# Where the operands of a split-float32 matmul lie in SBUF: two neighbouring x tiles in one block, high and low parts in blocks of their own, one distance to the weights modulo 256 bytes

## The chip, the cores and the metric

The kernel runs on one core of one Trainium2 chip. The metric is the device time of one execution in microseconds (us), the median of several runs. Nothing else runs on the chip's other cores.

## The reference

One inference step of a one-layer hybrid decoder trunk, 256 prompt tokens and 32 sample tokens (8 sequences of 4), model width 2048, float32 throughout. Both groups of tokens go through the same weights:

```
def swiglu(x, w_in, w_out):
    gate, up = jnp.split(x @ w_in, 2, axis=-1)
    return (jax.nn.silu(gate) * up) @ w_out
...
x = x + 0.5 * rmsnorm(swiglu(rmsnorm(x, g[0]), ffn1_w_in[l], ffn1_w_out[l]), g[1])
m, sg, sh = hybrid_mixer(rmsnorm(x, g[2]), mix_w_in[l], ..., mix_w_out[l], s_gla[l], s_hgrn[l])
x = x + rmsnorm(m, g[3])
x = x + 0.5 * rmsnorm(swiglu(rmsnorm(x, g[4]), ffn2_w_in[l], ffn2_w_out[l]), g[5])
```

The two feed-forward layers have 2048 x 11264 and 5632 x 2048 weights each. The mixer has an input projection of 7184 columns, two linear recurrences (gated linear attention and HGRN2), and an output projection of 2048 x 2048. The matrix products with these weights are nearly all of the arithmetic.

## The kernel before

**Layout.** Activations lie transposed: a tile `x{k}` holds 128 of the 2048 model features (partitions) by 288 tokens (256 prompt, 32 sample). There are 16 such tiles (KT = 16), and as many products along the contraction.

**Split float32.** TensorE multiplies in a rounded float32 form (`F32R`). To keep float32 accuracy each operand is split into a high part (the value rounded by a copy on ScalarE, ACT) and a low part (the remainder, by VectorE, DVE). A product of weight tile w and activation tile x is then three matmuls that add up in the same PSUM bank, in `mm3` of `block` (lines 617 to 619): w high by x high (L617), w high by x low (L618), w low by x high (L619). I call these three a triple, and one matmul a product. Each product has a weight load of its own (128 columns of 128 weights) and streams 288 columns of x. In all there are 16,152 such products: the groups `gate` and `up` (feed-forward input), `out` (feed-forward output, which streams the hidden parts `hp` instead of `xp`), and in the mixer `qk`, `v`, `hfq`, `hi`, `gate` and `mo`.

**Loops.** `block` runs over units of weights; a unit is 128 x 1024 weights, that is two neighbouring tiles k by 512 output columns. Within a unit it goes over four output groups f of 128 columns, and for each over the two k: so the triples run (k even, f 0), (k odd, f 0), (k even, f 1), (k odd, f 1), and so on: 24 products per unit. In the first blocks of each stage some units run with k outside (`byk`).

**Weights.** `Weights.load` brings a unit by one DMA of the SP queue into one of three raw buffers; `pieces` splits it, ACT writes the high part (L119), DVE the low part (L120), into a buffer `wh` of `[128, 2, 1024]`: for each k 512 high values, then 512 low values. There are four such buffers in the pool `hlp`. Around the borders between stages two more lie in an extra pool (`hx2`, `hx4`) at the right end of SBUF, and `wider` gives them every third pair of units there: 80 of the 1,408 triples of `out` and 144 triples of x tiles take their weights from these, counted in the built program.

**Activations as moving operand.** `pair` makes for each k a tile of `[128, 4, 2, 72]` values: the 288 tokens are cut into four places of 72, and in each place 72 high values are followed by 72 low values. `turns_of` makes the matmul read it in turns: 4 values (16 bytes) of place 0, 4 of place 1, of place 2, of place 3, then the next 4 of place 0. Two places lie 576 bytes apart, so the four reads of a turn lie 64 bytes apart modulo 256. The low part starts 288 bytes behind the high part, which is 32 modulo 256. `do_in` makes the same layout for four tiles of hidden units (`hp`).

**Gaps.** Small unused tiles (`gap_w`, `gap_f`, `{name}gap`, `gap{gnext}`) shift where the pools start. With them the start addresses are, modulo 256, in bytes: x high 64, x low 96; hidden high 192, hidden low 224; weights in `hlp` 96, in the extra pools 224. All x tiles are 2304 = 9 x 256 bytes, all weight offsets are multiples of 512, so these numbers hold for every k, f and buffer.

**Order.** The order of instructions on each engine is laid down by the kernel's code; TensorE goes through the products one after another, and loads the weights of the next product while it streams the present one.

Of the kernel before, what the change touches and what calls it, by code (L numbers as in the profile page):

```python
# [9 lines left out]
F32 = mybir.dt.float32  # L10
F32R = mybir.dt.float32r
# [5 lines left out]
P = 128  # L17
TP = 256
TS = 32
T = TP + TS  # L20
# [3 lines left out]
KT = D // P  # L24
# [6 lines left out]

RAW_BUFS = 3
HL_BUFS = 4
HALF = 1024
LINE = 4
PLACES = 4


def columns(t):

    return t.rearrange("p (g c) -> p g c", g=PLACES)
# [4 lines left out]
    return t.rearrange("p g (i e) -> p i g e", e=LINE)  # L46


def pair(pool, name):

    t = pool.tile([P, PLACES, 2, T // PLACES], F32R, name=name)
    return t[:, :, 0, :], t[:, :, 1, :]

SCAN_LAG = 4
X_EARLY = 12
# [2 lines left out]
class Weights:  # L58
# [46 lines left out]
    def pieces(self, n):  # L105

        i = self.split
        raw = self.raws.pop(i)
        pool = self.extra if i in self.extra_units else self.hlp
        hl = pool.tile([P, 2, HALF], F32R, name=f"wh{i}", tag="wh")  # L110
        h, l = hl[:, :, 0:512], hl[:, :, 512:1024]
        self.parts[i] = (h, l)
        self.split += 1
        raw = raw.rearrange("p (a b) -> p a b", b=512)
        for j in range(n):
            a = slice(0, 2) if n == 1 else slice(2 * j // n, 2 * j // n + 1)
            w = min(512, 1024 // n)
            c = slice(j * w % 512, j * w % 512 + w)
            i1 = self.nc.scalar.activation(h[:, a, c], raw[:, a, c], AF.Copy).ins  # L119
            i2 = self.nc.vector.tensor_tensor(l[:, a, c], raw[:, a, c], h[:, a, c].bitcast(F32), op=ALU.subtract).ins  # L120
            self.recent = i1, i2
            yield i1, i2
# [27 lines left out]
def trunk_kernel(ctx, tc, x_prompt, x_sample, state_gla, state_hgrn, norm_gains, f1_in, f1_out, f2_in, f2_out,  # L150
# [6 lines left out]
    xpool = ctx.enter_context(tc.tile_pool(name="xpool", bufs=1))  # L157
    rawp = ctx.enter_context(tc.tile_pool(name="rawp", bufs=RAW_BUFS))
    hlp = ctx.enter_context(tc.tile_pool(name="hlp", bufs=HL_BUFS))
    hlp.tile([P, 24], F32, name="gap_w", bufs=1)  # L160
    mmp = ctx.enter_context(tc.tile_pool(name="mmp", bufs=5, space=PSUM))
    aux = ctx.enter_context(tc.tile_pool(name="aux", bufs=3, space=PSUM))
    sqp = ctx.enter_context(tc.tile_pool(name="sqp", bufs=2))
# [18 lines left out]
    def act(out, in_, func, **kw):  # L182
        act_set(func)
        ins = S.activation(out, in_, func, **kw).ins
        order(ins, cur["load"])
        cur["users"].append(ins)
        return ins
# [39 lines left out]
    def wider(n):  # L227

        return {i for i in range(n - 44, n + 4) if i // 2 % 3 == (n + 2) // 2 % 3}
# [37 lines left out]
    EARLY = 4  # L267
    x = [xpool.tile([P, T], F32, name=f"x{k}") for k in range(KT)]
    yg = [xpool.tile([P, 4, T], F32, name=f"y{k}") for k in range(4)]
    y = [yg[k // 4][:, k % 4, :] for k in range(KT)]  # L270
    xh, xl = zip(*(pair(xpool, f"xp{k}") for k in range(KT)))
    rt = xpool.tile([P, T], F32, name="rt")
    rp = xpool.tile([P, T], F32, name="rp")
    acc = xpool.tile([P, T], F32, name="acc")
# [223 lines left out]
    class PreNorm:  # L498
# [3 lines left out]
        def __init__(self, name, update, ahead, at):  # L502

            self.name, self.update, self.ahead, self.at, self.late = name, update, ahead, at, []
            self.tmps = None
# [25 lines left out]
    class Fill:  # L531
# [2 lines left out]

        def __init__(self, pool, name, gains, gnext, some, ahead):
            self.gnext, self.name, self.some, self.ahead = gnext, name, some, ahead
            pool.tile([P, 24], F32, name=f"{name}gap")

            self.tiles = [[pair(pool, f"{name}{n}{k}") for k in range(EARLY)] for n in "xy"]
            self.gains = pool.tile([P, 48], F32, name=f"{name}g")[:, 0:EARLY]  # L540
            V.tensor_tensor(self.gains, gains[:, 0:EARLY], prm[:, gnext * KT:gnext * KT + EARLY], op=ALU.mult)

        def old(self):
# [136 lines left out]
    def ffn(tag, gcol, gnext, pn, before, fill=None):  # L680
# [2 lines left out]
        border = []  # L683
        with ExitStack() as pools:
            fp = pools.enter_context(tc.tile_pool(name=f"ffn{tag}", bufs=2))
            fp.tile([P, 8], F32, name=f"gap_f{tag}", bufs=1)
            hid, final_tiles = {}, []

            def do_in(c):
                hp = fp.tile([P, 4, PLACES, 2, T // PLACES], F32R, name=f"hp{tag}_{c}", tag="hp")  # L690
                hh, hl = ([hp[:, f, :, j, :] for f in range(4)] for j in range(2))
                hid[c] = (hh, hl)
                gs = []

                def gate(g):
                    def run():
                        V.tensor_tensor(g, g, rt, op=ALU.mult)
                        act(g, g, AF.Silu)
                    return run

                def ev_gate(f, ps):
                    g = fp.tile([P, T], F32, name="g", tag="g", bufs=6)
                    gs.append(g)
                    if c == 0:
                        W.behind = S.activation(g, ps, AF.Copy).ins
                        pn.late.append(gate(g))
                    else:
                        V.tensor_tensor(g, ps, rt, op=ALU.mult)
                        act(g, g, AF.Silu)

                def ev_up(f, ps):
                    u = fp.tile([P, T], F32, name="u", tag="u", bufs=3)
                    ins = V.tensor_tensor(u, ps, rt, op=ALU.mult).ins  # L713
                    V.tensor_tensor(u, u, gs[f], op=ALU.mult)
                    S.activation(hh[f], columns(u), AF.Copy)
                    V.tensor_tensor(hl[f], columns(u), hh[f].bitcast(F32), op=ALU.subtract)
                    return ins

                if c == 0:
                    block(f"gate{tag}_0", KT, xrhs, ev_gate, tick=pn.tick0, most=1 if final else 0, fill=fill,  # L720
                          late=0 if final else FIRST, byk=range(KT))
                    before.close()
                    if not final:
                        border.append(Border(mixer_start, hg1, gnext, 5, 2))
                else:
                    block(f"gate{tag}_{c}", KT, xrhs, ev_gate, byk=(2,) if c == 1 else ())
                if final and c == 0:
                    last_pool()
                block(f"up{tag}_{c}", KT, xrhs, ev_up, tick=pn.tick1 if c == 0 else None,
                      byk=(0,) if c == 1 or final and c == 0 else (), lag=int(c == 0))  # L730
# [3 lines left out]
            def last_pool():  # L734

                zp = pools.enter_context(tc.tile_pool(name="last", bufs=1, side="right", reuse_waits="tile"))
                for n in ("z", "x"):
                    final_tiles.append((zp.tile([P, KT, 2, P], F32, name=f"{n}T"), zp.tile([P, D // 4], F32, name=f"{n}S")))
                final_tiles.append(zp)
# [92 lines left out]
            for kind, c, n in ffn_ops():  # L832
                do_out(c, n) if kind == "out" else do_in(c)
# [864 lines left out]
    class Border:  # L1698


        def __init__(self, n, gains, gnext, some, ahead=0):
            self.pools = ExitStack()
            top = self.pools.enter_context(tc.tile_pool(name=f"top{gnext}", bufs=1, side="right"))
            top.tile([P, 64], F32, name=f"gap{gnext}")
            W.begin_extra(self.pools.enter_context(tc.tile_pool(name=f"hx{gnext}", bufs=2, side="right")), wider(n))
            self.fill = Fill(self.pools.enter_context(tc.tile_pool(name=f"fl{gnext}", bufs=1, side="right")),
                             f"fill{gnext}", gains, gnext, some, ahead)

    pn = pre1 = PreNorm("pre1", x_first, FIRST, 11)
    pn.late.append(prm2)  # L1710
    u, border = ffn(1, lambda k: hg1[:, k:k + 1], 2, pn, first)
    u, border = mixer(PreNorm("pre2", u, UPDATED, 11), border)
    ffn(2, lambda k: hg1[:, KT + k:KT + k + 1], None, PreNorm("pre3", u, UPDATED, 11), border.pools, border.fill)


# [39 lines left out]
```

## Time and profile before

| | |
|---|---|
| time, median of 3 runs | 2179.05 us (2178.4 to 2179.31) |
| the profiled execution's own time | 2178.23 us |
| its span, first to last instruction | 2176.5 us |
| TensorE matmul (PE) busy | 2166.9 us |
| weight loads on TensorE (PEld) busy | 2148.0 us |
| VectorE (DVE), ScalarE (ACT) busy | 1384.1, 1017.8 us |
| DMA | 384.87 MB, mean 177 GB/s |

PE and PEld are two rows of one engine: loading the next weights overlaps the present product. [...] What a product costs is the spacing from its start to the next one's start; that is read from the times of the timeline, or from the count of matmuls in a stretch. A stretch's count includes those that began before it and had not ended: two, where matmuls of 290 ns follow each other every 127 to 129 ns.

### The profile page before, as it was taken

The page shows a single profiled execution, that of the slowest core. Times are in us where ns is not written, and L with a number is a line of the kernel's source. Part 1 is how long each engine was busy: PE and PEld are TensorE (multiplying, and loading weights), DVE is VectorE, ACT ScalarE, POOL GpSimd, SP SyncE. Part 2 cuts the span into 40 slices and gives each one's busy share as a digit, 9 for nine tenths or more (in the row PEclk, how much of TensorE's full clock was granted, in tenths as well). Part 3 has the DMA queues.
Part 4 walks back from the last instruction along what each step waited for, and adds up shares of the span by engine and source line. Part 5 has one row for each costly group of instructions (what it writes and reads, how often), then busy time and mean ns, then how long its engine had stood idle before and what let it go on. Part 6 is the DMA issues. An engine that isn't in the chain of part 4 may idle for free.

```text
span 2176.5 us, 43224 instructions
## 1 busy us (share of the span) xinstructions
PE 2166.9 (100%) x17828; PEld 2148.0 (99%) x17828; DVE 1384.1 (64%) x2253; ACT 1017.8 (47%) x1537; POOL 180.1 (8%) x327
## 2 busy tenths in 40 slices
PE   9999999999999999999999999999999999999999
PEld 9999999999999999999999999999999999999998
DVE  7645546554565568888888755844555466556656
ACT  6453333343334345655676654544333343333344
POOL 2000000000000001233110000000000020122005
PEclk9999999999999999999999999999999999999999
DMA  7655555555556654678566664555555565666555
GB/s 224 181 169 171 174 172 168 173 173 171 171 174 184 176 174 137 198 208 219 175 192 181 178 189 136 170 171 173 175 168 172 174 181 171 184 185 179 172 170 159
DMA packets 227334, 384.87 MB, mean 177 GB/s; under 512 B 21362, under 2 KB 60864, under 8 KB 227136
## 3 DMA queue, kind: packets, MB, share of 16 engines
q1 hardware_dynamic: 213872, 365.02, 56.6%
q0 software_dynamic: 10992, 16.77, 2.9%
q8 instruction: 140, 2.29, 0.4%
q10 hardware_dynamic: 2272, 0.31, 0.1%
q14 instruction: 58, 0.48, 0.1%
HBM read 363.75 MB, written 11.80 MB: 173 GB/s over the span
## 4 chain that ended last, share of the span: by engine, by line
PE 93%; DVE 3%; DMA 2%; ACT 1%; issue 1%; POOL 0%; ACTq 0%; DVEq 0%; POOLq 0%
PE gate L617 9%; PE gate L618 9%; PE gate L619 9%; PE out L619 8%; PE out L618 8%; PE out L617 8%; PE up L619 8%; PE up L618 8%; PE up L617 8%; PE hfq L617 1%; PE hfq L618 1%; PE hfq L619 1%; PE mo L617 1%; PE mo L619 1%; PE mo L618 1%; DVE wh L120 1%
## 5 line engine op out<-in xcount | busy, mean ns | idle before, releaser
L120 DVE TENSOR_TENSOR wh<-raw,wh 128x1024 fp32r<-128x1024 f32 (+1 forms) x676 | 821.8, 1217 | 591.1 <-ACT wh L119 590.1
L119 ACT ACTIVATE wh<-raw 128x1024 fp32r<-128x1024 f32 (+1 forms) x676 | 710.5, 1052 | 916.3 <-PE gate L619 286.1
L617 PE MATMUL gate<-xp,wh 128*128 128x288 f32 x1660 | 481.2, 291 | 0.5 <-DVE u L713 0.3
L619 PE MATMUL gate<-xp,wh 128*128 128x288 f32 x1660 | 477.5, 289 | 0.0
L618 PE MATMUL gate<-xp,wh 128*128 128x288 f32 x1660 | 476.4, 289 | 0.1
L617 PE MATMUL out<-hp,wh 128*128 128x288 f32 x1408 | 410.9, 292 | 0.0
L618 PE MATMUL out<-hp,wh 128*128 128x288 f32 x1408 | 409.7, 291 | 0.0
L619 PE MATMUL out<-hp,wh 128*128 128x288 f32 x1408 | 409.3, 291 | 0.0
L617 PE MATMUL up<-xp,wh 128*128 128x288 f32 x1408 | 408.1, 290 | 0.0
L619 PE MATMUL up<-xp,wh 128*128 128x288 f32 x1408 | 406.4, 289 | 0.0
L618 PE MATMUL up<-xp,wh 128*128 128x288 f32 x1408 | 406.3, 289 | 0.0
L618 PEld LDWEIGHTS gate<-xp,wh 128*128 128x128 f32 x1660 | 311.1, 188 | 1.0 <-DVE xp L283 0.7
L617 PEld LDWEIGHTS gate<-xp,wh 128*128 128x128 f32 x1660 | 310.6, 187 | 1.4 <-issue 0.5
L619 PEld LDWEIGHTS gate<-xp,wh 128*128 128x128 f32 x1660 | 310.8, 188 | 0.2 <-DVE wh L120 0.2
L619 PEld LDWEIGHTS out<-hp,wh 128*128 128x128 f32 x1408 | 265.5, 189 | 0.0
L618 PEld LDWEIGHTS out<-hp,wh 128*128 128x128 f32 x1408 | 264.9, 188 | 0.0
L618 PEld LDWEIGHTS up<-xp,wh 128*128 128x128 f32 x1408 | 264.7, 188 | 0.0
L617 PEld LDWEIGHTS out<-hp,wh 128*128 128x128 f32 x1408 | 263.9, 187 | 0.3 <-DVE y L804 0.3
L619 PEld LDWEIGHTS up<-xp,wh 128*128 128x128 f32 x1408 | 264.0, 187 | 0.0
L617 PEld LDWEIGHTS up<-xp,wh 128*128 128x128 f32 x1408 | 263.7, 187 | 0.0
L804 DVE TENSOR_TENSOR y<-out,y 128x288 f32<-128x288 f32 x287 | 120.6, 452 | 80.1 <-PE out L619 79.7
L761 POOL DMA_DIRECT2D xT<-b x64 | 37.1, 586 | 746.7 <-PE gate L619 558.9
(417 smaller groups left out, 2549.7 us busy)
## 6 DMA issues: line engine op xcount, KB each, us to landing
raw<-in_ffn_w_in_dram SPq DMA_DIRECT2D x350, 512.0 KB, 3.7
raw<-in_ffn_w_out_dram SPq DMA_DIRECT2D x176, 512.0 KB, 3.7
raw<-in_mix_w_in_dram SPq DMA_DIRECT2D x64, 512.0 KB, 4.3
raw<-in_mix_w_in_dram SPq DMA_DIRECT2D x96, 256.0 KB, 3.3
raw<-in_mix_w_out_dram SPq DMA_DIRECT2D x32, 512.0 KB, 3.6
out_dram<-s POOLq DMA_DIRECT2D x32, 256.0 KB, 3.1
s<-in_state_gla_dram SPq DMA_DIRECT2D x16, 256.0 KB, 5.9
s<-in_state_hgrn_dram SPq DMA_DIRECT2D x16, 256.0 KB, 5.7
```

What stands on the lines that cost most here:

```text
L119: i1 = self.nc.scalar.activation(h[:, a, c], raw[:, a, c], AF.Copy).ins
L120: i2 = self.nc.vector.tensor_tensor(l[:, a, c], raw[:, a, c], h[:, a, c].bitcast(F32), op=ALU.subtract).ins
L617: yield lambda: PE.matmul(dst, w[0][:, a, c], parts[0], start=start, stop=False)
L618: yield lambda: PE.matmul(dst, w[0][:, a, c], parts[1], start=False, stop=False)
L619: yield lambda: PE.matmul(dst, w[1][:, a, c], parts[0], start=False, stop=stop)
L761: queues[n % len(queues)].dma_start(dst[q * TS:(q + 1) * TS, 4 * g:4 * g + 4, :, cols].rearrange("p k t c -> p (k t) c"), b32[rows, q])
L804: V.tensor_tensor(y[k], ps, y[k], op=ALU.add)
```

## The change

The change gives the parts of x, of the hidden units and of the tiles for the stage borders (`Fill`) another layout, and pads the weight buffers.

- `pairs` takes the place of `pair`. All high parts of n tiles lie in one block, all low parts in a second block behind it. Two neighbouring tiles, k even and k odd, share a piece of 2304 bytes: in each of the four places 72 values of the even tile, then 72 values of the odd tile. The low block starts 16 bytes further modulo 256 than the high block.
- The weight buffer's row for one k grows from 1024 to 1032 values (`HALF`), so that the odd k's weights lie 32 bytes further modulo 256, as the odd x tile does.
- The gap tiles get other sizes.

| start modulo 256 bytes | before | after |
|---|---|---|
| low part minus high part, same tile | 32 | 16 |
| weights minus x high, weights in `hlp` / extra | 32 / 160 | 96 / 96 |
| weights minus hidden high, in `hlp` / extra | 160 / 32 | 96 / 96 |
| weights minus the low part, in the same order | 0 / 128, 128 / 0 | 80 / 80, 80 / 80 |
| next triple's weights minus this x high, k even to odd | as above | 128 |
| the same, k odd to even | as above | 64 |

```diff
-HALF = 1024
+HALF = 1024 + 8
...
-def pair(pool, name):
-
-    t = pool.tile([P, PLACES, 2, T // PLACES], F32R, name=name)
-    return t[:, :, 0, :], t[:, :, 1, :]
+def pairs(pool, n, names):
+
+    parts = []
+    for at, name in zip((0, LINE), names):
+        t = pool.tile([P, n * T + 16 * at], F32R, name=name, tag=name.split("_")[0])[:, at:at + n * T]
+        t = t.rearrange("p (k g j c) -> p k g j c", g=PLACES, j=2, c=T // PLACES)
+        parts.append([t[:, k // 2, :, k % 2, :] for k in range(n)])
+    return parts
...
-        hl = pool.tile([P, 2, HALF], F32R, name=f"wh{i}", tag="wh")
+        hl = pool.tile([P, 2112], F32R, name=f"wh{i}", tag="wh")[:, 0:2 * HALF].rearrange("p (a c) -> p a c", a=2)
...
-    hlp.tile([P, 24], F32, name="gap_w", bufs=1)
+    hlp.tile([P, 40], F32, name="gap_w", bufs=1)
...
-    xh, xl = zip(*(pair(xpool, f"xp{k}") for k in range(KT)))
+    xh, xl = pairs(xpool, KT, ("xh", "xl"))
...
-            pool.tile([P, 24], F32, name=f"{name}gap")
-
-            self.tiles = [[pair(pool, f"{name}{n}{k}") for k in range(EARLY)] for n in "xy"]
-            self.gains = pool.tile([P, 48], F32, name=f"{name}g")[:, 0:EARLY]
+            pool.tile([P, 8], F32, name=f"{name}gap")
+
+            self.tiles = [list(zip(*pairs(pool, EARLY, (f"{name}{n}h", f"{name}{n}l")))) for n in "xy"]
+            self.gains = pool.tile([P, 24], F32, name=f"{name}g")[:, 0:EARLY]
...
-            fp.tile([P, 8], F32, name=f"gap_f{tag}", bufs=1)
+            fp.tile([P, 24], F32, name=f"gap_f{tag}", bufs=1)
...
-                hp = fp.tile([P, 4, PLACES, 2, T // PLACES], F32R, name=f"hp{tag}_{c}", tag="hp")
-                hh, hl = ([hp[:, f, :, j, :] for f in range(4)] for j in range(2))
+                hh, hl = pairs(fp, 4, (f"hh{tag}_{c}", f"hl{tag}_{c}"))
...
-            top.tile([P, 64], F32, name=f"gap{gnext}")
+            top.tile([P, 80], F32, name=f"gap{gnext}")
```

The instructions of every engine, their order and their shapes stay the same; addresses differ. One wait is new. On POOL (GpSimd), where the mixer's scratch is set up (`it`, `vs` and `ahl` are scratch tiles, `mi` and `bm` masks), the rows of before are:

```order
L974 DMA mi_9570<-in_masks_dram 128x576 [waits DMASW0_49,PE_49]
L975 DMA bm_9571<-in_masks_dram 96x8 [waits DMASW1_49]
L977 MEMSET it 128x256
L977 MEMSET vs_9300 128x512
L977 MEMSET vs_9298 128x512
```

and in the changed kernel, three lines further down the file:

```order
L977 DMA mi_9563<-in_masks_dram 128x576 [waits DMASW0_49,PE_49]
L978 DMA bm_9564<-in_masks_dram 96x8 [waits DMASW1_49]
L980 MEMSET it 128x256
L980 MEMSET vs_9293 128x512 [waits PE_49]
L980 MEMSET vs_9291 128x512
```

The first `vs` memset now waits for TensorE as the mask DMA three rows ahead of it does, since the scratch tile overlaps another part of the border's tiles.

## The prediction, before the run

> **What bounds the kernel.** I read the page's busy times first, then the chain that ended last, then what TensorE's products are spaced at.
>
> ```profile
> span 2176.5 us, 43224 instructions
> PE 2166.9 (100%) x17828; PEld 2148.0 (99%) x17828; DVE 1384.1 (64%) x2253; ACT 1017.8 (47%) x1537; POOL 180.1 (8%) x327
> PEclk9999999999999999999999999999999999999999
> PE 93%; DVE 3%; DMA 2%; ACT 1%; issue 1%; POOL 0%; ACTq 0%; DVEq 0%; POOLq 0%
> ACT wh L119 <- PE gate L619: 286.1, 147, 2.0
> ```
>
> TensorE is busy all the time, at the full granted clock, and holds 93% of the chain. The last row, from the list of waits, says that the engine that prepares weights waits for products to give buffers back, not the other way round. So the time is the number of products times their spacing, and whatever changes the spacing by one part in a hundred changes the time by nearly as much. The groups of TensorE give the count (here L617, the first of three lines of equal count):
>
> ```profile
> L617 PE MATMUL gate<-xp,wh 128*128 128x288 f32 x1660 | 481.2, 291 | 0.5 <-DVE u L713 0.3
> L617 PE MATMUL out<-hp,wh 128*128 128x288 f32 x1408 | 410.9, 292 | 0.0
> L617 PE MATMUL up<-xp,wh 128*128 128x288 f32 x1408 | 408.1, 290 | 0.0
> L617 PE MATMUL hfq<-xp,wh 128*128 128x288 f32 x256 | 76.0, 297 | 0.0
> L617 PE MATMUL mo<-xp,wh 128*128 128x288 f32 x256 | 74.6, 291 | 0.1
> L617 PE MATMUL hi<-xp,wh 128*128 128x288 f32 x128 | 37.8, 296 | 0.0
> L617 PE MATMUL v<-xp,wh 128*128 128x288 f32 x128 | 37.8, 295 | 0.0
> L617 PE MATMUL qk<-xp,wh 128*128 128x288 f32 x124 | 34.4, 294 | 0.2 <-ACT xp L282 0.2
> ```
>
> With the 16 products of `Fill` these are 5,384 triples, 16,152 products. Now their spacing, from stretches that hold whole blocks (columns: the stretch, its length, PE busy and matmuls, clock, DMA share, GB/s):
>
> ```profile
> 502.75:551.68 48.93, 48.93 (x386) 1.00 0.57 172
> 551.68:576.48 24.80, 24.80 (x194) 1.00 0.57 170
> 576.48:625.45 48.97, 48.97 (x386) 1.00 0.58 172
> 718.03:724.15 6.12, 6.12 (x50) 1.00 0.61 173
> 724.15:773.31 49.16, 49.16 (x387) 1.00 0.58 172
> ```
>
> The first is one `gate` and one `up` block: 386 less the two that began before is 384 products in 48.93 us, 127.4 ns each. The third is the next such pair, 127.5. The second is four `out` blocks, 192 products in 24.80 us: 129.2 ns. Shapes and engines' load differ little; what differs is that x stands 32 bytes below its weights (modulo 256) and the hidden parts 160. The fourth stretch tells these apart: it is an `out` block whose weights lie in the extra pool, distance 32, and 48 products take 6.12 us, 127.5 ns. The fifth is the mirror image: `gate` and `up` with three in eight of their units in the extra pool, distance 160: 384 products in 49.16 us, 128.0, close to 5/8 of 127.5 and 3/8 of 129.2. So **the distance of the weights from the moving operand modulo 256 sets the spacing**, 127.5 ns at 32 and 129.2 at 160, for either operand.
>
> [...]
>
> **Part 1: one distance for all.** Products now at 160 go to the common distance: 1,408 - 80 = 1,328 triples of `out` and 144 of x, 1,472 triples or 4,416 products. If the new distance were as good as 32, each would gain 129.2 - 127.5 = 1.7 ns: 4,416 x 1.7 = 7.5 us. Nothing lies beside it: TensorE is the path.
>
> **Part 2: what the new distance is worth.** The trace has no product at 96 and 80. Its nearest rows are those of `Fill`, whose parts stand 64 below the weights; four triples from the timeline's first to the next block's first product:
>
> ```profile
> 1349.46 0.29 PE L617 MATMUL fill<-fill4y,wh 128*128 128x288 f32 x1
> ...
> 1350.86 0.30 PE L619 MATMUL fill<-fill4y,wh 128*128 128x288 f32 x1
> 1351.00 0.29 PE L617 MATMUL gate<-xp,wh 128*128 128x288 f32 x1
> ```
>
> Eleven steps in 1.40 us are 127.3 ns, twelve in 1.54 are 128.3: 64 is about as good as 32. The layout changes a second thing, which the steps within a stretch bear on:
>
> ```profile
> 510.02 0.29 PE L617 MATMUL gate<-xp,wh 128*128 128x288 f32 x1
> 510.15 0.29 PE L618 MATMUL gate<-xp,wh 128*128 128x288 f32 x1
> 510.27 0.29 PE L619 MATMUL gate<-xp,wh 128*128 128x288 f32 x1
> 510.40 0.29 PE L617 MATMUL gate<-xp,wh 128*128 128x288 f32 x1
> 510.53 0.29 PE L618 MATMUL gate<-xp,wh 128*128 128x288 f32 x1
> 510.66 0.29 PE L619 MATMUL gate<-xp,wh 128*128 128x288 f32 x1
> 510.78 0.29 PE L617 MATMUL gate<-xp,wh 128*128 128x288 f32 x1
> 510.91 0.29 PE L618 MATMUL gate<-xp,wh 128*128 128x288 f32 x1
> 511.04 0.29 PE L619 MATMUL gate<-xp,wh 128*128 128x288 f32 x1
> 511.16 0.29 PE L617 MATMUL gate<-xp,wh 128*128 128x288 f32 x1
> ```
>
> Over three triples the steps from L617 to L618 add to 0.39 us, from L618 to L619 to 0.38, from L619 to the next L617 to 0.37: about 130, 127 and 123 ns, each known to 3 ns by the rounding. The first two stay in one piece of 2304 bytes (a tile's high and low part), the last goes to another tile, and is the shortest. In the changed layout it is the other way round: high and low lie in blocks of their own, so two of three steps leave the piece, while the step from one triple to the next mostly stays in the piece that even and odd tile share. I take 125.5 for a step that leaves (between 123 and 127) and 129.3 for one that stays (between 127 and 130): (2 x 125.5 + 129.3) / 3 = 126.8 ns.
>
> **Bounds:** from 125 ns for all (near the shortest kind of step) to 129.2 (all as at 160). Against 127.5 that is, for 16,152 products, from -40 to +27 us. I take 126.8, -11 us: both nearest rows, 64 and 32, are on the good side, and the share of steps that leave the piece doubles.
>
> **The rest costs nothing.** ACT and DVE write the same elements in rows of another pitch:
>
> ```profile
> L120 DVE TENSOR_TENSOR wh<-raw,wh 128x1024 fp32r<-128x1024 f32 (+1 forms) x676 | 821.8, 1217 | 591.1 <-ACT wh L119 590.1
> L119 ACT ACTIVATE wh<-raw 128x1024 fp32r<-128x1024 f32 (+1 forms) x676 | 710.5, 1052 | 916.3 <-PE gate L619 286.1
> ```
>
> A unit's 24 products take 24 x 127.5 ns = 3.06 us; its split takes 1.05 us on ACT and 1.22 on DVE. If the new addresses made these even a fifth slower, some 0.2 us per unit, the products would still cover it; without that cover 0.2 us on each of 676 pieces would be 135 us. The new wait of POOL's memset is for products that the mask DMA three rows ahead waits for too, at the mixer's border; behind it stand one memset and the loads of the gate weights, and POOL is busy 8% of the span. SP's queue gets nothing new, and at 57% share the DMAs have room for products that come 1% sooner.
>
> **Sum.** The profiled execution took 2178.2 us (span 2176.5 and 1.7 around it). 2178.2 - 7.5 - 11.3 = 2159.4. The median of before is 0.8 us above that execution, so I say **2160 us**, 0.9% faster.
>
> **Rivals.**
> - *The distance 128 decides (slower).* From an even tile to the odd one, the next weights now lie 128 beyond the x that is being streamed. That is the distance of the low parts in `out`, in the stretch at 129.2 ns; and none of the new ones (96, 80, 64) is 32 or 0. If this and the unknown pair cost all products what 160 and 128 cost, the time is 2178.2 + 16,152 x 1.7 ns - 4,416 x 1.7 ns = 2198. It turns to a loss when the mean spacing passes 127.5 + 7.5 us / 16,152 = 128.0 ns. Against it: `Fill` at 64. Chance 0.22.
> - *Nothing happens.* [...] By chance the new spacing may also be 127.7 to 128.2. Together 0.13.
> - *Only part 1.* The new distance is as good as 32 and no better: 2178.2 - 7.5 = 2170.7. Chance 0.2.
> - *All steps become short.* 125 to 126 ns everywhere: 2130 to 2147. Chance 0.1.
> - *The change doesn't do what it says.* 16 tiles of 1152 bytes are 18432 = 72 x 256, so the low block does start 16 bytes off, and 1032 values are 4128 = 16 x 256 + 32. I give this nothing of its own.
>
> My forecast, 126.2 to 127.3 ns or 2150 to 2168, has 0.35.
>
> **How the numbers follow.** Faster by over 0.2% (about what a measurement of this kernel can tell from no change; below 2174.7): the forecast, only part 1, and all short, 0.35 + 0.2 + 0.1 = 0.65. Same: 0.13. Slower: 0.22. The range leaves out the far half of the short case and the far end of the slow one: 2138 to 2197.
>
> **What would show it.** The stretches that hold whole blocks: `gate`, `up` and `out` must stand at one spacing, whatever pool the weights come from (part 1), and at about 126.8 ns (part 2); L617 to L618 must have become shorter, L619 to L617 longer. If the `out` stretch has gained and `gate` lost, the distance to the next weights decides, not the piece. If `gate` and `out` still differ, part 1 is wrong. An idle PE ahead of L617 with DVE or ACT as releaser would mean that the writes have become slower.

## The result, and the profile after

| | before | after |
|---|---|---|
| time, median | 2179.14 us (2178.4 to 2179.31, 4 runs) | 2159.28 us (2157.96 to 2159.76, 4 runs) |
| ratio, 95% interval | | 0.9909 [0.9891, 0.9926] |
| the profiled execution's own time | 2178.23 us | 2157.96 us |

The changed kernel is 0.9% faster: 19.9 us by the medians, 20.3 us between the two profiled executions. These are the rows of its page that answer to those of before: span and busy times, the granted clock in tenths, the chain that ended last, and the two groups that write the split weights (busy us, mean ns of one, idle time ahead).

```profile
span 2156.2 us, 43224 instructions
PE 2144.9 (99%) x17828; PEld 2126.5 (99%) x17828; DVE 1382.0 (64%) x2253; ACT 1017.1 (47%) x1537; POOL 180.6 (8%) x327
PEclk9999999999999999999999999999999999999999
PE 94%; DVE 3%; ACT 2%; DMA 1%; issue 1%; DVEq 0%; ACTq 0%; SPq 0%
L124 DVE TENSOR_TENSOR wh<-raw,wh 128x1024 fp32r<-128x1024 f32 (+1 forms) x676 | 822.1, 1217 | 579.9 <-ACT wh L123 577.7
L123 ACT ACTIVATE wh<-raw 128x1024 fp32r<-128x1024 f32 (+1 forms) x676 | 710.1, 1052 | 899.0 <-PE gate L623 282.5
```

TensorE is still the bound, at the same clock, and the writers take the same 1,217 and 1,052 ns as before. PE's busy time fell by 22.0 us and the span by 20.3: the gain is TensorE's alone. The stretches of whole blocks in the changed kernel (stretch, its length, PE busy and matmuls, clock, DMA share, GB/s), TensorE's rows only:

```profile
498.18:546.82 48.64, 48.64 (x386) 1.00 0.58 173
546.82:571.14 24.32, 24.32 (x194) 1.00 0.59 174
711.07:717.16 6.09, 6.09 (x51) 1.00 0.63 180
717.16:765.80 48.64, 48.64 (x387) 1.00 0.57 173
```

The first is a `gate` and an `up` block, 384 products in 48.64 us; the second four `out` blocks, 192 in 24.32; the third an `out` block from the extra pool, 48 in 6.09 (the ends are rounded to 0.01 us); the fourth `gate` and `up` with three in eight of their units in the extra pool. All stand at 126.7 ns (by its rounded row the third would have 126.9, by its start times it has 126.67), where before had 127.4, 129.2, 127.5 and 128.0. By the start times in the trace it is 126.66 to 126.68 ns in nearly every whole block of the feed-forward layers. Over all steps under 150 ns from one product to the next, the mixer's with them, the mean went from 128.08 to 126.81 ns, and the longer steps add up to 24 us in both kernels. 16,152 x 1.27 ns = 20.5 us is the whole gain.

The steps within the first stretch, from the timeline (L621, L622, L623 are the former L617, L618, L619):

```profile
498.18 0.29 PE L621 MATMUL gate<-xh,wh 128*128 128x288 f32 x1
498.31 0.29 PE L622 MATMUL gate<-xl,wh 128*128 128x288 f32 x1
498.44 0.29 PE L623 MATMUL gate<-xh,wh 128*128 128x288 f32 x1
498.56 0.29 PE L621 MATMUL gate<-xh,wh 128*128 128x288 f32 x1
498.69 0.29 PE L622 MATMUL gate<-xl,wh 128*128 128x288 f32 x1
498.82 0.29 PE L623 MATMUL gate<-xh,wh 128*128 128x288 f32 x1
498.94 0.29 PE L621 MATMUL gate<-xh,wh 128*128 128x288 f32 x1
```

Every triple takes 0.38 us here. The rows seem to say 130, 130 and 120 ns for the three kinds of step, but a triple of 380 ns is a whole number of 10 ns, so the same rounding error comes back in every triple. The trace's own start times give, over the 64 triples of this `gate` block, 127.3, 126.3 and 126.5 ns; for the block shown of before 128.6, 127.5 and 126.1.

### The profile page after: what moved, and what is told of

Its sections match the earlier page's. It is cut to its first block, busy times and chain, and to the rows that moved or that the text cites. A ratio compares the mean times of both kernels' runs of the same rounds, so it can differ in the third digit from the quotient of the medians.

```text
span 2156.2 us, 43224 instructions
## 1 busy us (share of the span) xinstructions
PE 2144.9 (99%) x17828; PEld 2126.5 (99%) x17828; DVE 1382.0 (64%) x2253; ACT 1017.1 (47%) x1537; POOL 180.6 (8%) x327
## 4 chain that ended last, share of the span: by engine, by line
PE 94%; DVE 3%; ACT 2%; DMA 1%; issue 1%; DVEq 0%; ACTq 0%; SPq 0%
PE gate L621 10%; PE gate L622 9%; PE gate L623 9%; PE out L621 8%; PE out L622 8%; PE out L623 8%; PE up L621 8%; PE up L622 8%; PE up L623 8%; PE hfq L621 2%; PE mo L621 1%; PE hfq L622 1%; PE hfq L623 1%; PE mo L623 1%; PE mo L622 1%; ACT wh L123 1%
## 5 line engine op out<-in xcount | busy, mean ns | idle before, releaser
L124 DVE TENSOR_TENSOR wh<-raw,wh 128x1024 fp32r<-128x1024 f32 (+1 forms) x676 | 822.1, 1217 | 579.9 <-ACT wh L123 577.7
L123 ACT ACTIVATE wh<-raw 128x1024 fp32r<-128x1024 f32 (+1 forms) x676 | 710.1, 1052 | 899.0 <-PE gate L623 282.5
L621 PE MATMUL gate<-xh,wh 128*128 128x288 f32 x1660 | 479.8, 290 | 0.6 <-ACT wh L123 0.4
L623 PE MATMUL gate<-xh,wh 128*128 128x288 f32 x1660 | 476.4, 288 | 0.0
L622 PE MATMUL gate<-xl,wh 128*128 128x288 f32 x1660 | 475.6, 289 | 0.1
L621 PE MATMUL up<-xh,wh 128*128 128x288 f32 x1408 | 406.8, 289 | 0.0
L621 PE MATMUL out<-hh,wh 128*128 128x288 f32 x1408 | 406.7, 289 | 0.0
L622 PE MATMUL up<-xl,wh 128*128 128x288 f32 x1408 | 405.9, 288 | 0.0
L622 PE MATMUL out<-hl,wh 128*128 128x288 f32 x1408 | 405.9, 288 | 0.0
L623 PE MATMUL up<-xh,wh 128*128 128x288 f32 x1408 | 405.8, 288 | 0.0
L623 PE MATMUL out<-hh,wh 128*128 128x288 f32 x1408 | 405.7, 288 | 0.0
L621 PEld LDWEIGHTS gate<-xh,wh 128*128 128x128 f32 x1660 | 311.0, 188 | 1.7 <-ACT wh L123 0.6
L622 PEld LDWEIGHTS gate<-xl,wh 128*128 128x128 f32 x1660 | 310.2, 188 | 1.1 <-DVE xl L287 0.8
L623 PEld LDWEIGHTS gate<-xh,wh 128*128 128x128 f32 x1660 | 311.0, 188 | 0.2 <-DVE wh L124 0.2
L623 PEld LDWEIGHTS up<-xh,wh 128*128 128x128 f32 x1408 | 264.3, 188 | 0.0
L623 PEld LDWEIGHTS out<-hh,wh 128*128 128x128 f32 x1408 | 264.3, 188 | 0.0
L621 PEld LDWEIGHTS out<-hh,wh 128*128 128x128 f32 x1408 | 264.2, 188 | 0.0
L621 PEld LDWEIGHTS up<-xh,wh 128*128 128x128 f32 x1408 | 264.2, 188 | 0.0
L622 PEld LDWEIGHTS up<-xl,wh 128*128 128x128 f32 x1408 | 264.1, 188 | 0.0
L622 PEld LDWEIGHTS out<-hl,wh 128*128 128x128 f32 x1408 | 264.0, 188 | 0.0
```

The costliest lines, as they stand in the source:

```text
L621: yield lambda: PE.matmul(dst, w[0][:, a, c], parts[0], start=start, stop=False)
L622: yield lambda: PE.matmul(dst, w[0][:, a, c], parts[1], start=False, stop=False)
L623: yield lambda: PE.matmul(dst, w[1][:, a, c], parts[0], start=False, stop=stop)
```

## The experiments

Two questions stood after the result. Is it the distance to the weights or the layout that pays? And why 126.67 ns? Where a spacing is given to a hundredth of a ns, it is worked out from the start times in the trace of that run. In the kernel's own variants nothing of the computation is left out; the five benchmarks compute nothing of the reference, and each ran once.

### One distance, old layout

Before, with the gaps alone changed, so that all weights lie 32 bytes above the high part and none at 160: part 1 without part 2.

```diff
-            fp.tile([P, 8], F32, name=f"gap_f{tag}", bufs=1)
+            fp.tile([P, 40], F32, name=f"gap_f{tag}", bufs=1)
...
-            top.tile([P, 64], F32, name=f"gap{gnext}")
+            top.tile([P, 32], F32, name=f"gap{gnext}")
```

> The kernel before with its old layout, but the gaps set so that all weights, in both pools, stand 32 bytes above x high and hidden high modulo 256 (part 1 alone; only the 48 products of Fill stand elsewhere). Distance theory (the distance of the next weights from the streamed operand sets the spacing): out falls from 129.2 to 127.5 ns, gate and up stay at 127.5, the time falls by 7.5 us to 2171. Piece theory (a step that stays in a piece of 2304 bytes is long, one that leaves it short): the layout is the old one, so by it alone nothing moves, 2178 to 2179.

Measured: 2169.97 us, ratio 0.9965 [0.9952, 0.9978]. The stretches (`gate` and `up`, then four `out` blocks):

```profile
501.18:550.10 48.92, 48.92 (x386) 1.00 0.58 173
550.10:574.57 24.47, 24.47 (x195) 1.00 0.56 172
```

127.4 ns in both. `out` has come from 129.2 to where `gate` stands, and `gate` hasn't moved: 7.6 us below the 2177.60 us that before had beside it, for which part 1 had 7.5.

### The new distance in the old layout, and the old distance in the new layout

The old layout with x at the new distance 96, the hidden parts at 32 (first diff), and the changed kernel with x at the old distance 32, the hidden parts at 96 (second). So each kernel holds two combinations side by side.

```diff
-    hlp.tile([P, 24], F32, name="gap_w", bufs=1)
+    hlp.tile([P, 40], F32, name="gap_w", bufs=1)
...
-            fp.tile([P, 8], F32, name=f"gap_f{tag}", bufs=1)
+            fp.tile([P, 40], F32, name=f"gap_f{tag}", bufs=1)
...
-            top.tile([P, 64], F32, name=f"gap{gnext}")
+            top.tile([P, 16], F32, name=f"gap{gnext}")
```

> The old layout (high and low of a tile in one piece, 32 apart), x at distance 96 (low parts 64), the hidden parts at 32 (low 0) in both pools. If the distance alone does it: gate and up fall from 127.5 to about 126.7 ns as in the changed kernel, out stands at 127.5, time 2160 to 2163. If the separate blocks do it: gate and up stay at 127.5, time 2171.

```diff
-    hlp.tile([P, 40], F32, name="gap_w", bufs=1)
+    hlp.tile([P, 24], F32, name="gap_w", bufs=1)
...
-            top.tile([P, 80], F32, name=f"gap{gnext}")
+            top.tile([P, 96], F32, name=f"gap{gnext}")
```

> The changed kernel with the x weights at distance 32 (low parts 16) in both pools instead of 96 and 80, hidden parts still at 96 and 80. If the distance does it: gate and up go back to 127.5 ns, out stays at 126.7, time about 2168 to 2170. If the separate blocks do it: all stay at 126.7, 2159.

Measured: 2176.11 us, ratio 0.9992 [0.9982, 1.0001], and 2181.59 us, ratio 1.0014 [1.0005, 1.0023]. Both are longer than either answer that was expected. The stretches of the first:

```profile
502.86:551.93 49.07, 49.07 (x386) 1.00 0.58 172
551.93:576.41 24.48, 24.48 (x195) 1.00 0.56 173
```

and of the second:

```profile
503.62:553.13 49.51, 49.51 (x387) 1.00 0.57 170
553.13:577.47 24.34, 24.34 (x194) 1.00 0.58 174
```

| spacing in these stretches | weights 32 above high | weights 96 above high |
|---|---|---|
| old layout | 127.4 to 127.5 ns | 127.8 ns, in other blocks 128.9 |
| new layout | 128.9 ns | 126.7 to 126.8 ns |

The first variant's blocks of x stand at two spacings. A `gate` block early in the first layer has 128.9 ns, a later one, whose products read the very same addresses, 127.8:

```profile
134.71:159.46 24.75, 24.75 (x195) 1.00 0.59 170
208.67:233.21 24.54, 24.54 (x194) 1.00 0.58 172
```

Neither half of the change pays alone: the new distance in the old layout loses 0.4 or 1.4 ns, the old distance in the new layout loses 1.5, both together gain 0.7. The kinds of step say more. In the old layout at 96 the step from L619 to L617, which leaves the piece of 2304 bytes, became the longest (129.6 ns in the mean over all steps of x, against 126.4 at 32), although the pieces are those of before. In the new layout at 32 the step from L622 to L623 became 132.1 ns, where the changed kernel has 126.7, though both leave the piece. So a step isn't long or short by the piece.

### Two maps

A benchmark of products alone, with the changed kernel's layout in one unit. The first goes through 16 distances from high to low part (s) by 16 from high part to weights (d), 48 products each, the second lets the start of x and of the weights move on from product to product. The first in short:

```
for s in range(16):
    for d in range(16):
        xh, xl = x_at(72 * k), x_at(1024 + 4 * s + 72 * k)     # 4 values = 16 bytes
        weights at 4 * d + 1032 * k
```

> Not the reference's work: products alone, in the changed kernel's layout, 48 for each of 16 distances of weights to high part (0 to 240 bytes) and 16 of low to high part (0 to 240), 256 cells one after the other; the outputs hold no result. Distance theory: the spacing varies from cell to cell between about 125 and 130 ns, with 126.7 at weights 96 and low 16, and has its slow cells where a distance is 128 to 160. Piece theory: all cells within 0.5 ns of each other, since all have separate blocks.

> Not the reference's work: products alone, in 256 cells of 48; in a cell every product's moving operand starts a fixed step further than the one before (0 to 240 bytes modulo 256, by 16: the rows) and so do its weights (0 to 240: the columns). New theory (slots): the moving operand's four places are served in turn, one per 1.667 ns, so a product that starts at the same place as the one before can only start after whole turns of 6.667 ns, 19 turns are 126.67 ns, and a start 192 bytes further comes one slot earlier, 125.0 ns, one 64 further one slot later, 128.3; rows differ then by their step in multiples of 64, and columns hardly. Distance theory: what counts is the distance of the next weights, so cells on the diagonal (equal steps, constant distance 96) are alike at about 126.7 whatever the step, and cells off it spread to 130. Were neither so, all cells would be at one value.

The first map (the mean of each cell's last 36 steps) runs, without its very first cell, from 126.7 to 132.3 ns, with a mean near 129.4. Its rows for s = 16 and 32 bytes (ns, d in steps of 16 bytes from 0):

```
s=16  129.6 129.8 128.9 128.7 130.8 127.9 127.8 130.6 128.9 126.8 128.9 129.0 130.0 129.2 130.1 127.8
s=32  127.7 129.3 130.4 128.8 129.3 128.9 129.4 127.8 130.0 130.4 128.4 128.9 129.2 129.7 129.6 129.9
```

The distance d alone orders nothing, and no neighbourhood is good: 16 bytes up or down change these rows by up to 3 ns. The cell s = 16, d = 32 stands at 128.9 ns, as the variant with these distances did. But the changed kernel's own cell, d = 96, stands at 127.8 and not at 126.67. That was a miss, and it opened the third question: the same distances can give two spacings.

In the second map, products that all read the same addresses modulo 256 stand at 126.7 ns (this is the first cell, and its last 24 steps alone are taken); when x and weights both move on by 64 bytes a product it is 128.33, by 128 bytes 130.0. A move of 64 bytes, one of the four places, thus costs 1.7 ns in these two cells. A move by 192, for which 125.0 was expected, gave an irregular 128.7, and one other cell stands at 125.4 (x on by 208, weights by 80), so it isn't a rule for the whole map. The turn of 6.667 ns in that expectation, a nineteenth of 126.67, and the 1.667 of a place, a quarter of a turn, are the author's estimates from the measured spacing; that the places are served in turn isn't shown.

### How lasting is a pattern?

The changed kernel's distances, 32 times, each behind 12 products with other addresses, with one unit's addresses and then with the kernel's steps from unit to unit; behind that, coarse maps for two orders of the triple, the present one (high by high, high by low, low by high) and the one with the last two exchanged.

> Not the reference's work: products alone. One and two: the changed kernel's distances 32 times within one unit, and 32 times with the kernel's steps from unit to unit, 96 products each, each behind 12 products of another pattern. If the same distances hold two lasting patterns (the scan of distances stood at 127.8 ns where the kernel stands at 126.7), both sections show cells of both kinds; if address bits above 256 bytes decide, section two stands at 126.7 alone and section one at 127.8. Three and four: 512 cells of 24 products each by low to high (s), odd to even tile (q) and weights to high (d), in the order high-high, high-low, low-high, then in the order high-high, low-high, high-low. Slot theory: a triple in the first order returns to the place where it began, so no cell of it goes below 126.7 for long; in the second order starts can go backwards all the time, and the cells with s 192, q 128 come to about 125.6. Distance theory: no order is better than the other, both have their best cells at the same distances.

31 of 32 and 32 of 32 cells settled at 126.67 to 126.71 ns within 48 products; one stayed at 127.75. So two patterns exist for these addresses, and the kernel's is by far the likelier. In the present order no cell of 512 is below 126.56 ns; in the exchanged order one is, at 125.61 (low 192 bytes behind high, weights 64 above).

### The exchanged order in the changed kernel

```diff
-            yield lambda: PE.matmul(dst, w[0][:, a, c], parts[1], start=False, stop=False)
-            yield lambda: PE.matmul(dst, w[1][:, a, c], parts[0], start=False, stop=stop)
+            yield lambda: PE.matmul(dst, w[1][:, a, c], parts[0], start=False, stop=False)
+            yield lambda: PE.matmul(dst, w[0][:, a, c], parts[1], start=False, stop=stop)
...
```

> The changed kernel with its layout, each triple in the order high-high, low-high, high-low instead of high-high, high-low, low-high (the sum in PSUM is the same but for rounding). Slot theory: the starts shift by 0, 16 and 16 or -48 bytes and come back after two triples, so the floor stays 126.67 ns and the time 2159 at best; where weights now collide it is longer, up to 2185. If the order of itself were better (the same x streamed twice in a row), all blocks fall below 126.6 ns and the time below 2157.

Measured: 2189.23 us, ratio 1.005 [1.0033, 1.0067], longer than the 2185 that was expected at most; 128.9 ns in all whole blocks of the feed-forward layers. The stretch of `gate` and `up`:

```profile
506.73:556.23 49.50, 49.50 (x387) 1.00 0.56 170
```

With no address changed, the order of three products is worth 2.2 ns each: what counts is the sequence of addresses, not a distance within one product.

### In search of 125.6

A finer map of the exchanged order, with pairs whose start alternates, and then a kernel whose layout has the one good cell's distances.

> Not the reference's work: products alone. One: a layout of slots of 288 bytes in which the starts go backwards by 64 bytes at two of three products (high even, low even, high odd, low odd at 0, 192, 128, 64), pairs of tiles in turn 32 bytes apart, in the order high-high, low-high, high-low, then in the order high-high, high-low, low-high; 16 distances of weights to high, by 16 bytes, four units each. Slot theory: in the first order the best distances stand at about 125.6 ns (a cycle of six products saves one turn of 6.667 ns against six times 126.67: 126.67 - 6.667 / 6 = 125.56), in the second none is below 126.6. Two: the first order with s, q and the distance in steps of 16 bytes around s 192, q 128: cells near 125.6 where the starts go round backwards once in six products, 126.7 or more elsewhere. Distance theory: the orders do not differ.

125.6 ns came in two cells of 400 (low 176 with weights 160, low 192 with weights 64), the next best is 126.6. With alternating starts the best is 126.93 in the exchanged order, where 125.6 was expected, and 128.5 in the present one.

> The whole computation in the order high-high, low-high, high-low, with the starts of the moving operand going backwards: high even, low even, high odd, low odd of a pair at 0, 192, 128, 64 modulo 256, weights 64 beyond their high part everywhere. The first eight x tiles stand in the even slots of 288 bytes, the last eight in the odd ones 32 bytes further (their weights too), and the hidden chunks take even and odd slots in turn, so that the 32 bytes come once or twice per block of 192 products and not once per unit. Slot theory: 125.6 ns in most of a block and some triples at 127 to 129 after each change of slots, mean 125.6 to 126.2, time 2178 - 7.5 - 16,152 x (127.5 - 125.9) ns = 2145, 2140 to 2152. Distance theory: 64 from the high part is as good as 32, 127.4 ns, 2171. If the lock seen in cells of 24 to 48 products does not hold beside the other engines, blocks stand at 127 to 129, 2165 to 2190.

Measured: 2201.96 us, ratio 1.0114 [1.0095, 1.0132], a clear miss. The stretch of `gate` and `up`, and the four `out` blocks behind it:

```profile
509.18:559.39 50.21, 50.21 (x386) 1.00 0.56 168
559.39:583.51 24.12, 24.12 (x195) 1.00 0.58 175
```

These `out` blocks do run at 125.6 ns; but the `out` blocks 75 us earlier and 74 us later, whose addresses lie 32 bytes further modulo 256, stand at 131.1, and those 150 us earlier, with the very same addresses of x and weights, at 131.0. Two patterns again, and here the bad one is the likelier.

> Not the reference's work: products alone, in the order high-high, low-high, high-low with the odd tile 128 beyond the even one and the low part 176 or 192 beyond the high one; for each of 16 distances of the weights ten cells of 72 products, each behind 12 products of another pattern. If a distance holds more than one lasting pattern, its ten cells fall into groups (for 192 and 64 near 125.6 and near 131, as in the kernel with backward starts, whose out blocks stood at 125.6 twice and at 131 else); a distance whose ten cells all stand at 125.6 would make a kernel of about 2145. If the start does not matter and the other engines made the 131, all ten cells at 192 and 64 stand at 125.6.

Ten starts from other addresses for each distance. Low 192, weights 64: 131.0 ns five times, 129.9 to 130.0 four times, 125.6 once. Low 176, weights 160: 125.6 nine times, 128.7 once. Low 192, weights 0 or 128: 126.6 to 126.7 ten times of ten. The last 36 products of two starts at low 176 and weights 160, one of each pattern:

```profile
1149.80:1154.32 4.52, 4.52 (x38) 1.00 0.00 0
1160.53:1165.17 4.64, 4.64 (x39) 1.00 0.00 0
```

The same 36 products on the same addresses of x and weights, 4.52 or 4.64 us (125.56 and 128.7 ns by the start times), with no DMA beside them. Where the results go doesn't decide it: they go to PSUM banks in a cycle of four starts, and the second and tenth start have the banks of the sixth, the one at 128.7, and stand at 125.6. In the program the 12 products ahead are the only difference left. That they decide it, and not chance, isn't shown, since each start ran once.

> The whole computation in the order high-high, low-high, high-low, with the odd tile 128 beyond the even one, the low part 176 beyond the high one, weights 160 beyond the high part everywhere: the relation at which nine of ten cells stood at 125.6 ns and one at 128.7. Pairs stand 0 or 64 bytes (whole places) further, their weights too, and 32 further in the second half of the x tiles and in every other hidden chunk. Slot theory with two lasting patterns: most blocks at 125.6 to 125.9 ns, some at 128.7, time 2178 - 7.5 - 16,152 x (127.5 - 125.9) ns = 2145, 2140 to 2160. If the steps between pairs upset the pattern: 127 to 129 ns, 2163 to 2190. Distance theory: 160 is the bad one, 129.2, 2198.

Measured: 2186.08 us, ratio 1.0036 [1.0023, 1.005]: not the 2145 us of the theory, but the second of the three cases, that the steps between pairs upset the pattern. The stretch of `gate` and `up`, and the four `out` blocks behind it:

```profile
504.86:554.14 49.28, 49.28 (x386) 1.00 0.57 171
554.14:578.85 24.71, 24.71 (x194) 1.00 0.57 171
```

It is 128.3 to 128.7 ns in `gate` and `up`, and 128.7 and 129.0 by turns in `out`. In this layout a step to another pair of tiles moves all addresses by 64 or 32 bytes; triples of 376 to 378 ns, that is 125.6 a product, show only for parts of a unit, until the next such step.

### Padded, so that no step changes the distances

The order is the exchanged one again. Here every tile of x and of the hidden units has low 176 and weights 160, and no step to another pair moves the addresses; the places of a pair are spread over 1280 bytes. From the even to the odd tile x and weights move by 128 bytes, as in the benchmark (the expectation says 32 by mistake). The rows of x grow, and one of the four split weight buffers is given up for it (the diff is against before).

```diff
-HL_BUFS = 4
-HALF = 1024
+HL_BUFS = 3
+HALF = 1024 + 32
...
+    t = pool.tile([P, PLACES * (160 * n + 16)], F32R, name=name, tag=name.split("_")[0]).rearrange("p (g c) -> p g c", g=PLACES)
+
+    def part(k, at):
+        return t[:, :, 320 * (k // 2) + at:320 * (k // 2) + at + T // PLACES]
+    return [[part(k, at[k % 2]) for k in range(n)] for at in ((0, 160), (236, 76))]
```

> The last kernel ran the order w high x high, w low x high, w high x low with the low part 176 bytes behind the high part modulo 256 and the weights 160 beyond, and each step to another pair of tiles moved all addresses by 64 or 32 and threw it out of its pattern. Here the places of a pair are padded so that every tile has the same low distance 176 and weight distance 160; only the start differs from the even to the odd tile, by 32. The price is wider weight rows, for which one of four split weight buffers is given up. The theory of turns that can settle in a lasting pattern: the benchmark with these distances stood at 125.6 ns in 9 of 10 starts, so most blocks at 125.6 to 126 ns, a triple at 377 to 378 ns: some 2140 to 2155 us, faster than the changed kernel; if the other pattern of the benchmark holds, 128.7 ns and about 2190 us. The rival, that every change of addresses breaks the pattern, whatever the padding: 128 to 129 ns, as in the last kernel, 2180 to 2190 us. With one buffer fewer, waits of TensorE for ACT or DVE would show as idle time ahead of the first product of a unit, and add to either.

Measured: 2184.53 us median, ratio 1.0046 [1.0022, 1.007], where 2140 to 2155 was expected, and from 2170.31 to 2206.12 us in ten runs, where before spreads over 3 us. The profiled execution is the fastest of them. Its stretches (`gate` and `up`, four `out` blocks), and then four that make up the whole span: to the mixer's first product, the mixer, the first three blocks of the second feed-forward layer, and the rest.

```profile
494.87:543.08 48.21, 48.21 (x386) 1.00 0.58 175
543.08:567.19 24.11, 24.11 (x195) 1.00 0.57 175
...
0.00:809.28 809.28, 807.11 (x6396) 806.46 (x6397) 472.31 (x664) 347.88 (x444) 14.93 (x35) 1.00 0.59 178
809.28:1344.08 534.80, 524.36 (x5040) 510.38 (x5039) 416.84 (x854) 319.13 (x645) 89.22 (x158) 0.99 0.62 181
1344.08:1429.00 84.92, 78.60 (x589) 77.67 (x589) 63.94 (x110) 45.52 (x75) 0.00 (x0) 0.96 0.49 144
1429.00:2168.50 739.50, 733.63 (x5809) 730.21 (x5807) 428.49 (x628) 303.85 (x376) 76.40 (x134) 1.00 0.60 178
```

The same four in the changed kernel (columns as above: PE, PEld, DVE, ACT and POOL, each with its count):

```profile
0.00:814.43 814.43, 812.67 (x6396) 811.79 (x6397) 476.27 (x666) 351.38 (x447) 14.94 (x35) 1.00 0.60 179
814.43:1334.77 520.34, 517.94 (x5040) 504.02 (x5039) 416.33 (x855) 319.63 (x645) 89.23 (x158) 1.00 0.64 186
1334.77:1412.00 77.23, 76.88 (x596) 75.87 (x596) 62.11 (x109) 43.65 (x74) 0.00 (x0) 1.00 0.50 148
1412.00:2156.20 744.20, 737.36 (x5802) 734.77 (x5801) 427.24 (x626) 302.44 (x373) 76.46 (x134) 1.00 0.60 176
```

In this execution the feed-forward layers hold 125.56 ns in nearly every block: the first layer is 5.15 us shorter than in the changed kernel, the last stretch 4.7. The mixer and the blocks behind its border give back 14.5 and 7.7 us, of which 8.0 and 6.0 are more idle time of TensorE. It waits there for split weights, which it hardly does in the changed kernel (0.4 us for ACT's half in all); two rows from the list of waits (us in total, times, longest):

```profile
PE qk L628 <- DVE wh L130: 5.7, 3, 4.6
PE gate L628 <- DVE wh L130: 5.1, 1, 5.1
```

and the granted clock is 0.96 in the stretch that holds the second of these. The rest, 6.4 us in the mixer and 1.7 behind it, is longer busy time for about as many matmuls. In part that is the clock, which stands at 0.50 for 3.4 us twice in the mixer; but the good pattern doesn't hold there either: the mixer's steps under 150 ns have a mean of 128.0 ns, against 127.1 in the changed kernel. That the lost buffer is the cause of the waits is argued from the releaser, not shown by a run; why the pattern fails in the mixer isn't shown; nor is it shown what the slower nine executions did, since they left no trace. A layout with this pattern and four buffers wasn't tried. No version beats the changed kernel.

## Why the prediction came out

The time said was 2160 us, the time measured 2159.28. Step by step:

- **What bounds the kernel.** Right. The gain is the count of products times the change of their spacing, 20.5 us against 20.3.
- **Part 1, one distance for all, 7.5 us.** Right, and shown by itself: 7.6 us with the gaps alone. But that the distance sets the spacing holds for 32 and 160 in the old layout and no further: at 32 the new layout has 128.9 ns.
- **Part 2, 126.8 ns, 11.3 us.** The size was right: 126.67 ns in whole blocks, 126.81 over all clean steps. From one distance to the changed kernel the ratio falls from 0.9965 to 0.9909, 0.56% or 12.2 us.
- **The reason given for part 2 was wrong.** The step that failed is "I take 125.5 for a step that leaves and 129.3 for one that stays". In the `gate` block above the two kinds that leave stand at 127.3 and 126.3 ns, and 56 steps that stay in the piece at 126.6: no such two kinds exist. What the forecast said would show it, L617 to L618 shorter and L619 to L617 longer, holds by sign alone: 1.3 ns shorter where 4.5 was forecast (130 to 125.5), and 0.4 longer where 6.3 was (123 to 129.3). The two runs that took distance and layout apart gave long steps where the piece asked for short ones.
- **Why the number held all the same.** By luck: the mean of assumed 125.5, 125.5 and 129.3 happened to lie near 126.67. The input was weak: three steps of each kind, read in rows of 0.01 us, gave 130, 127 and 123 ns, where the block's 64 triples have 128.6, 127.5 and 126.1. "Known to 3 ns" was true, and a difference of 7 ns built on it was one of 2.5.
- **The rest at nothing.** Right: the split's two groups kept their durations, the sum of disturbed steps is 24 us in both kernels, and the new wait of POOL costs nothing. Its timeline in the changed kernel shows the memset of `vs` right behind that of `it`, with no idle time ahead:

```profile
839.10 0.33 POOL L980 MEMSET it<- 128x256 f32 x1
839.36 1.01 POOL L980 MEMSET vs<- 128x512 f32 x2
```

- **The rival that 128 decides.** Not here: the step from L623 to L621 has distance 128 from even to odd tile and stands at 126.8 ns, as does the one at 64. But its fear was a fair one: a loss was one gap away, since the new layout with x at 32 is 0.14% slower than before.
- **The rival that nothing happens.** Ruled out. That a shift of addresses is worth nothing doesn't hold for these products: with instructions, shapes, order and the places of the results untouched, moving the weights of x by 64 bytes is worth 2.2 ns a product in the new layout (128.9 against 126.7).
- **Only part 1; all steps short.** The first fell with the 12.2 us. The second, 125 to 126 ns, does exist, as the padded kernel shows, but in another order of the three and not at these addresses.

What is shown is that the spacing hangs on the sequence of addresses modulo 256, of x and of weights, over a whole triple and into the next (the weights of x moved alone: 128.9 against 126.7 ns; the order alone: 2.2 ns); that one such sequence can hold more than one spacing (125.6 and 128.7 ns); that the changed kernel's settles at 126.67 ns nearly always (63 of 64 starts in the benchmark, where steps by whole multiples of 256 bytes from unit to unit made no difference); and that this takes layout and distance together. Which step of the new layout does it (low parts 16 bytes on, odd tiles and their weights 32) wasn't taken apart, and why the addresses count isn't shown.

## What to carry to other kernels

Where TensorE is the bound and its spacing differs between groups of one shape, look at the start addresses modulo 256 of both operands: here whole blocks stood between 125.6 and 131.1 ns, for no instruction more or less. Measure a layout with its distance, in the kernel: for x, the new distance alone and the new layout alone both made the products longer (127.8 or 128.9 ns, and 128.9, from 127.4), and a benchmark's cell may settle in another pattern than the kernel does (127.8 against 126.67). And don't build a mechanism on three rows of a rounded timeline; average over a block.

## What the runs showed of the hardware

- The repeats measured for 128 x 288 products in this form fit one grid. The triples' patterns repeat after 1520 ns in the changed kernel (four triples), 1146.7 ns in before at distance 32 (three) and 2713.3 ns at 160 (seven), worked out from the start times. All three are whole multiples of 6.667 ns (228, 172 and 407), and 126.67 ns is 19 times that. The 6.667 ns is an estimate from these repeats; what makes such a grid isn't shown. The lowest spacing of a whole block in any kernel here is 125.56.
- The same products on the same addresses have more than one lasting pattern (4.52 against 4.64 us for 36 of them, with nothing else on the core), and in the program only what ran before differs. In a kernel that shows as blocks of equal shape at two spacings, 125.6 and 131.1 ns, and may be why the padded kernel's times spread over 36 us.
- Idle time went with a lower clock: in the stretch behind the mixer's border TensorE idles 6.3 of 84.9 us in the padded kernel at a mean granted clock of 0.96, and 0.4 of 77.2 us in the changed one at 1.00. In the padded kernel the clock is 0.50 from 1358.27 to 1365.10 us; a wait of 5.1 us had begun 3.3 us before. Soon after a wait of 1.2 us at 1055.05 it is 0.50 for 3.4 us too, but after another of 1.2 us at 1268.06 it stays at 1.00, so no limit can be read from this run.
